# The first norm's shift and scale in four steps of two chunks each, on one core

## The chip, the cores and the metric

The kernel runs on one core of a Trainium2 chip. The metric is the device time of one execution in microseconds (us). It was run three times: 2135.63, 2139.49 and 2140.38 us, a median of 2139.49. One more execution was recorded by the hardware profiler; all rows below are from it.

## The reference

Two blocks follow one another; the change lies at the very start of the first. There a vector per stream (x and ctx) is turned into shifts and scales by a dense layer with 6144 outputs, the input is normed, scaled and shifted, and then multiplied by the mixer's input weights:

```python
m = jax.nn.silu(cvec) @ w_ada[:, :n * D_MODEL] + b_ada[:n * D_MODEL]
sh1, sc1, gt1, sh2, sc2, gt2 = jnp.split(m, 6, axis=-1)      # per stream
hx = rms_norm(h_x, g_mix) * (1.0 + sc1) + sh1                 # 256 x 1024, the same for ctx
proj = hx @ w_in                                              # 1024 x 2576
```

`D_MODEL` is 1024, x and ctx have 256 rows each. Only `sh1` and `sc1`, the first 2048 of the 6144 outputs, are needed for this first norm. Behind it follow a depthwise convolution, a state-space scan, an output projection and a mixture of experts, twice, and then a second block of four layers.

## The kernel before, in words

Features lie on the 128 partitions, so a stream is 8 chunks of 128 features by 256 rows; x and ctx stand side by side, 512 columns.

Shift and scale come from `w_ada` in units (`ada`, L200). A unit is one load of 1 MiB, 128 rows of `w_ada` by 2048 outputs, rows of 8 KB, and four fp32 matmuls (`adaps`) of 32 output rows by 512 columns that lie beside each other in the array; only two of the 32 rows are used (the two streams). Eight units add up to one block of 2048 outputs, and the first block is `sh1` and `sc1`. Then `turn` copies the sums from PSUM to `adar`, transposes them (`adat`) and makes `AD` (the vectors with their bias) and `A` (1 + scale, times the norm's gain). There are three blocks per layer and two layers, 48 units; `fill(n)` works off the next n of them, and its calls lie all over the first block wherever TensorE had room.

`load_x` (L162) loads the parameters, starts the first units, loads x and ctx, sums the squares (`ssq`, by matmuls with ones) with further units between them, takes root and reciprocal (`rs`), and works off the eighth unit and `turn`.

`mixer` (L304) loads the small `wd` weights and the first two pieces of `w_in`. All weights come by SyncE's queue into the tag `raw`, which has five buffers of 1 MiB: a load waits until the tile that had the buffer before has been read for the last time. Weights are split for fp32r into `wh` (ScalarE, L54) and `wl` (VectorE, L55). `modulated` (L279) then goes over the 8 chunks: times `rs` (`nrm`), times `A` plus `AD` (`nrmf`; VectorE for x, ScalarE for ctx), split into `xh` and `xl`. With each chunk `first` issues eight matmuls of 512 columns: two for `tmw`, and three each for the two projections that are open. These are the 64 first-stage matmuls. Further projections and the convolutions follow.

The order within each engine is made by a scheduler from the order of the program and priorities, and is fixed when the kernel is built; an engine takes its instructions in that order. It also hands out the `raw` buffers as they come free.

Of the kernel before, what the change touches and what calls it, by code (L numbers as in the profile page):

```python
# [7 lines left out]
F32 = mybir.dt.float32  # L8
# [3 lines left out]
AF = mybir.ActivationFunctionType  # L12
ALU = mybir.AluOpType
# [3 lines left out]
P = 128  # L17
D = 1024
KC = D // P
# [10 lines left out]
class Net:  # L30
# [100 lines left out]
    def block1(self):  # L131
        nc, tc, i = self.nc, self.tc, self.i
        with ExitStack() as c1:
            self.c1p = c1.enter_context(tc.tile_pool(name="consts1", bufs=1))
            self.consts()
            cb = ExitStack()
            self.big = cb.enter_context(tc.tile_pool(name="big", bufs=1))
            self.hs = [self.x, self.big.tile([P, KC, T], F32, name="hc")]
            self.AD = [self.c1p.tile([P, 48, 2], F32, name=f"AD{l}") for l in range(2)]
            self.A = [self.c1p.tile([P, 2, KC, 2], F32, name=f"A{l}") for l in range(2)]  # L140
            self.PV = [None, None]
            self.adar = self.c1p.tile([P, 4, P], F32, name="adar")
            self.turns, self.units = [], 0
            self.adag = [self.ada(0), self.ada(1)]
            self.moe_dram(c1, 2 * T)
            for l in range(2):
                with ExitStack() as c2:
                    self.tmp = c2.enter_context(tc.tile_pool(name="tmp", bufs=1))
                    self.pm = c2.enter_context(tc.tile_pool(name="pm", bufs=8, space=PSUM))
                    self.mmtag, self.t2b = "mm", 5  # L150
                    if l == 0:
                        self.load_x()
                    self.mixer(l)
                    if l:
                        self.setup2()
                if l == 0:
                    self.moe0(128)
            cb.close()
            self.b8p = self.ctx.enter_context(tc.tile_pool(name="b8", bufs=1, side="right"))
            self.moe1()  # L160

    def load_x(self):  # L162

        nc, i = self.nc, self.i
        c16 = self.params(0)
        sc = self.tmp.tile([P, 16], F32, name="silc")
        nc.scalar.activation(sc, c16, AF.Silu)
        self.sc32 = self.c1p.tile([P, KC, 32], F32, name="sc32")
        nc.gpsimd.memset(self.sc32, 0.0)
        nc.vector.tensor_copy(self.sc32[:, :, 0:2], sc.rearrange("p (s k) -> p k s", s=2))  # L170
        self.fill(2)
        for s, name in enumerate(("x", "ctx")):
            nc.sync.dma_start(self.hs[s], i[name])
        self.ssq_begin(2)
        for k in range(KC):
            self.ssq_add(k)
            if k % 2:
                self.fill(1)
        r = self.rs1 = self.rsn[:, :2 * T]
        nc.scalar.activation(r, self.ssq, AF.Sqrt, bias=self.eps[:, 0:1], scale=1.0 / D)  # L180
        with self.tc.high_priority(offset=-60):
            for q in range(4):
                nc.vector.reciprocal(r[:, q * P:q * P + P], r[:, q * P:q * P + P])
        self.fill(2)
        self.ada_flush()

    def params(self, l):

# [11 lines left out]
    def ada(self, l):  # L200

        nc, i = self.nc, self.i
        w = i["w_ada"][l].rearrange("(k p) n -> p k n", p=P)
        AD, A, rows = self.AD[l], self.A[l], self.adar

        def turn(b):  # L210
            pv = self.PV[l]
            pt = self.pm.tile([P, 4, P], F32, name="adat", tag=self.mmtag)
            for j in range(4):
                nc.tensor.transpose(pt[:, j], rows[:, j], self.ident)
            pt = pt.rearrange("p j (a r) -> p a j r", r=32)
            o = AD[:, 16 * b:16 * b + 16].rearrange("p (a j) s -> p a j s", j=4)
            for a in range(4):
                nc.vector.tensor_tensor(o[:, a], pt[:, a, :, 0:2], pv["b_ada"][:, 16 * b + 4 * a:16 * b + 4 * a + 4, None].to_broadcast([P, 4, 2]), op=ALU.add)
            if b != 1:
                n, at, gn = (0, 8, "g_mix") if b == 0 else (1, 32, "g_ffn")  # L220
                nc.vector.scalar_tensor_tensor(A[:, n], AD[:, at:at + 8], 1.0, pv[gn][:, :, None].to_broadcast([P, 8, 2]),
                                               op0=ALU.add, op1=ALU.mult)

        for b in range(3):
            ps, taken = None, False
            for k in range(KC):
                self.ada_flush()
                first = ps is None
                if first:
                    ps = self.pm.tile([P, 512], F32, name="adaps", tag=self.mmtag)  # L230
                r = self.raw(w[:, k, 2048 * b:2048 * b + 2048].rearrange("p (g n) -> p g n", n=512), 4, 512)
                for a in range(4):
                    self.mm(ps[32 * a:32 * a + 32], self.sc32[:, k], r[:, a], first, k == KC - 1)
                if k == KC - 1 or self.hold:
                    o = rows.rearrange("p j n -> p (j n)")
                    if taken:
                        nc.vector.tensor_tensor(o, o, ps, op=ALU.add)
                    else:
                        nc.scalar.activation(o, ps, AF.Copy)
                    ps, taken = None, True  # L240
                if k == KC - 1:
                    self.turns.append((turn, b))
                yield
# [32 lines left out]
        self.nc.scalar.activation(r, self.ssq, AF.Sqrt, bias=self.eps[:, 0:1], scale=1.0 / D)  # L276
        self.nc.vector.reciprocal(r, r)

    def modulated(self, l, which, streams, out_f=None, each=None, xs=None):  # L279

        nc = self.nc
        n = T * streams
        r = self.rs1
        xh, xl = xs or (self.b16("xh"), self.b16("xl"))
        for k in range(KC):
            t = self.tmp.tile([P, n], F32, name="nrm", tag="t2", bufs=self.t2b)
            f = self.tmp.tile([P, n], F32, name="nrmf", tag="t2", bufs=self.t2b) if out_f is None else out_f[:, k, :n]
            for s in range(streams):
                sl = slice(s * T, s * T + T)
                shift, scale = self.vec(l, 3 * which, k, s), self.A[l][:, which, k, s:s + 1]  # L290
                (nc.gpsimd if s else nc.vector).tensor_tensor(t[:, sl], self.hs[s][:, k], r[:, sl], op=ALU.mult)
                if s:
                    nc.scalar.activation(f[:, sl], t[:, sl], AF.Identity, bias=shift, scale=scale)
                else:
                    nc.vector.tensor_scalar(f[:, sl], t[:, sl], scale, shift, op0=ALU.mult, op1=ALU.add)
            self.split(xh[:, k, :n], xl[:, k, :n], f, nc.gpsimd if streams == 1 else None)
            if each:
                each(k, xh, xl)
        return xh, xl
# [1 line left out]
    def b16(self, name, dt=F32R, shape=None):  # L301
        return self.big.tile(shape or [P, KC, 2 * T], dt, name=name, tag="b16", bufs=5)

    def mixer(self, l):  # L304
        nc, i = self.nc, self.i
        last = l == 1
        NS = 1 if last else 2
# [10 lines left out]
        pt = self.pm.tile([32, 4 * P], F32, name="tmw", tag="mm")  # L318

        def first(k, xh, xl):  # L320
            self.mm(pt, wd[:, k], xh[:, k], k == 0, False)
            self.mm(pt, wd[:, k], xl[:, k], False, k == KC - 1)
            for q in range(2):
                self.mm3(p0[q], w0[q][0][:, k], w0[q][1][:, k], xh[:, k, :NX], xl[:, k, :NX], k == 0, k == KC - 1)
        xh, xl = self.modulated(l, 0, 2, each=first)
        pv = self.PV[l]

        pd = self.turned(pt, 16, 4, self.pm, self.tmp, "mm")
# [3 lines left out]
        a = self.tmp.tile([P, 16], F32, name="aneg")  # L332
# [31 lines left out]
        for c in range(4):  # L364
            b = c % 2
# [9 lines left out]
        for a in range(4):  # L375
            r = self.raw(win[:, :, 1536 + 256 * a:1792 + 256 * a], KC, 256)
            for b in range(2):
                c = 2 * a + b
# [34 lines left out]
            for k in range(k0, k1):  # L413
                self.mm3(ps[m], ws[m][0][:, k], ws[m][1][:, k], mh[:, k, :NX], ml[:, k, :NX], k == 0, k == KC - 1)
        if last:
            self.fill(48 - self.units, True)
            self.ada_flush()
        for m in range(3):
            wout(m, 0, 4)
# [182 lines left out]
    def ssd(self, l, xbc, xdt, cz, dt, dta, rows, NS, ssq, conv, cnorm):  # L602
# [116 lines left out]
        while todo or live or later:  # L719
            if todo:  # L720
                live.insert(0, head(n, *todo.pop(0)))
            live = [g for g in live if next(g, self) is not self]
            while sums:
                sums.pop(0)()
            if next(before, self) is self and later:
                s, c = later.pop(0)
                if s == 0:
                    carry(c)
                sums.append(finish(s, c))
            if n < half:  # L730
                conv(8)
            elif n == half:
                conv(1000)
            else:
                next(cnorm, None)
            if l == 0 and n in (12, 14):
                self.fill(1, n == 14)
            if l == 1 and self.units < 48:
                self.fill(1, self.units == 47)
            n += 1  # L740
        for f in sums:
            f()
# [1548 lines left out]
```

## Time and profile before

| | |
|---|---|
| median of 3 runs | 2139.49 us |
| the profiled execution | 2133.34 us, span 2131.5 us |
| TensorE (PE) busy | 1963.7 us, 92% of the span |
| VectorE (DVE) busy | 1472.7 us, 69% |
| ScalarE (ACT) busy | 1036.9 us, 49% |
| mean DMA rate | 192 GB/s |
| granted TensorE clock, mean | 0.967 of 2.4 GHz |

Shares over the whole span tell little of the change, which lies in the first 55 us. To read it one goes by stretches: which engine is full in which, and what ended the idle time ahead of the first matmuls of each kind. A clock of 0.50 is 1.2 GHz, 1.00 is 2.4 GHz. In the timeline a row merges instructions of one kind that follow one another (x8: eight of them), and an fp32 matmul leaves two records, an fp32r matmul one.

### The profile page before, as it was taken

The page shows a single profiled execution, that of the slowest core. Times are in us where ns is not written, and L with a number is a line of the kernel's source. Part 1 is how long each engine was busy: PE and PEld are TensorE (multiplying, and loading weights), DVE is VectorE, ACT ScalarE, POOL GpSimd, SP SyncE. Part 2 cuts the span into 40 slices and gives each one's busy share as a digit, 9 for nine tenths or more (in the row PEclk, how much of TensorE's full clock was granted, in tenths as well). Part 3 has the DMA queues.
Part 4 walks back from the last instruction along what each step waited for, and adds up shares of the span by engine and source line. Part 5 has one row for each costly group of instructions (what it writes and reads, how often), then busy time and mean ns, then how long its engine had stood idle before and what let it go on. Part 6 is the DMA issues. An engine that isn't in the chain of part 4 may idle for free.

```text
span 2131.5 us, 37017 instructions
## 1 busy us (share of the span) xinstructions
PE 1963.7 (92%) x14915; PEld 1696.5 (80%) x14915; DVE 1472.7 (69%) x2429; ACT 1036.9 (49%) x1742; POOL 437.1 (21%) x574
## 2 busy tenths in 40 slices
PE   6999786999889879799999997899999999999998
PEld 3666465998666656378889996799999999989998
DVE  4999558998796541089866679875558556767554
ACT  4335635886634521066554451354455444655444
POOL 1001202234251110113279812200010000010000
PEclk9999997999999989999999998899999999999999
DMA  7665236999326579955555552355544554436551
GB/s 304 232 207 172 82 103 221 346 339 335 109 73 236 178 245 368 378 173 179 172 185 184 198 177 93 110 187 189 192 138 153 190 191 161 139 108 218 189 179 40
DMA packets 275571, 408.89 MB, mean 192 GB/s; under 512 B 9856, under 2 KB 241280, under 8 KB 268096
## 3 DMA queue, kind: packets, MB, share of 16 engines
q1 hardware_dynamic: 265952, 380.47, 52.5%
q0 software_dynamic: 8000, 19.67, 2.6%
q10 hardware_dynamic: 1440, 6.29, 0.7%
q8 instruction: 120, 1.97, 0.4%
q14 instruction: 59, 0.48, 0.1%
HBM read 390.93 MB, written 24.64 MB: 195 GB/s over the span
## 4 chain that ended last, share of the span: by engine, by line
PE 48%; DVE 9%; DMA 2%; issue 2%; ACT 1%; POOL 1%; SPq 0%; DVEq 0%; POOLq 0%; ACTq 0%
PE mm L46 43%; DVE wl L55 2%; PE gu L46 2%; PE py L46 1%; DVE Z L2137 1%; DMA rawe<-in_w_down 1%; PE px L46 1%; DVE gl L1533 1%; DMA raw<-in_w_down 1%; DVE A L2130 0%; PE mm L1766 0%; DVE A L2139 0%; DVE s5a L2088 0%; POOL Z L2132 0%; DMA bc<-bcd 0%
## 5 line engine op out<-in xcount | busy, mean ns | idle before, releaser
L54 ACT ACTIVATE wh<-raw 128x1024 fp32r<-128x1024 f32 x490 | 511.2, 1050 | 477.8 <-PE mm L46 262.5
L55 DVE TENSOR_TENSOR wl<-raw,wh 128x1024 fp32r<-128x1024 f32 (+2 forms) x478 | 586.7, 1233 | 211.8 <-ACT wh L54 209.7
L46 PE MATMUL mm<-gh,wh 128*128 128x256 f32 (+1 forms) x1744 | 496.1, 285 | 1.0 <-ACT wh L54 1.0
L46 PE MATMUL mm<-gh,wl 128*128 128x256 f32 (+1 forms) x1744 | 493.0, 283 | 2.3 <-DVE wl L55 2.3
L46 PE MATMUL mm<-gl,wh 128*128 128x256 f32 (+1 forms) x1744 | 492.8, 283 | 0.5 <-DVE gl L1533 0.5
L46 PEld LDWEIGHTS mm<-gh,wh 128*128 128x128 f32 (+1 forms) x1744 | 329.0, 189 | 4.1 <-issue 1.8
L46 PEld LDWEIGHTS mm<-gh,wl 128*128 128x128 f32 (+1 forms) x1744 | 328.5, 188 | 3.7 <-DVE wl L55 3.0
L46 PEld LDWEIGHTS mm<-gl,wh 128*128 128x128 f32 (+1 forms) x1744 | 328.7, 188 | 2.3 <-DVE gl L1533 0.9
L46 PE MATMUL mm<-fh,wh 128*128 128x256 f32 x704 | 198.4, 285 | 3.1 <-DVE x L1573 1.6
L46 PE MATMUL mm<-fl,wh 128*128 128x256 f32 x704 | 198.8, 283 | 0.2 <-DVE fl L55 0.2
L46 PE MATMUL mm<-fh,wl 128*128 128x256 f32 x704 | 198.1, 283 | 0.0
L1537 POOL TENSOR_TENSOR sq<-sq 128x256 f32<-128x256 f32 x48 | 41.2, 859 | 682.2 <-ACT sq L1535 483.3
L46 PEld LDWEIGHTS mm<-fh,wh 128*128 128x128 f32 x704 | 133.6, 191 | 5.1 <-DVE x L1573 2.4
L46 PEld LDWEIGHTS mm<-fl,wh 128*128 128x128 f32 x704 | 134.7, 191 | 0.7 <-DVE fl L55 0.6
L46 PEld LDWEIGHTS mm<-fh,wl 128*128 128x128 f32 x704 | 134.5, 191 | 0.0
L46 PE MATMUL proj<-xh,wl 128*128 128x512 f32 (+1 forms) x320 | 117.6, 368 | 10.7 <-POOL xr L518 8.8
L46 PE MATMUL proj<-xh,wh 128*128 128x512 f32 (+1 forms) x320 | 119.3, 373 | 1.6 <-ACT wh L54 1.6
L46 PE MATMUL proj<-xl,wh 128*128 128x512 f32 (+1 forms) x320 | 116.3, 364 | 0.0
L46 PE MATMUL gu<-wh,gt 128*128 128x256 f32 x512 | 98.6, 286 | 0.2 <-DVE gt L55 0.2
L1599 DVE TENSOR_TENSOR ft<-mm,rstd 128x512 f32<-128x512 f32 x88 | 60.8, 691 | 51.0 <-PE mm L46 51.0
L54 ACT ACTIVATE fh<-fa 128x256 fp32r<-128x256 f32 x88 | 36.7, 417 | 111.6 <-DVE fa L1602 111.6
L46 PEld LDWEIGHTS proj<-xh,wh 128*128 128x128 f32 x320 | 63.1, 197 | 29.6 <-issue 15.9
(596 smaller groups left out, 4112.7 us busy)
## 6 DMA issues: line engine op xcount, KB each, us to landing
raw<-in_ffn_w_gate_up SPq DMA_DIRECT2D x88, 1024.0 KB, 5.4
raw<-in_w_ada SPq DMA_DIRECT2D x48, 1024.0 KB, 6.0
raw<-in_ffn_w_down SPq DMA_DIRECT2D x44, 1024.0 KB, 4.8
raw<-in_fox_w_in SPq DMA_DIRECT2D x24, 1024.0 KB, 6.2
raw<-in_w_down SPq DMA_DIRECT2D x22, 1024.0 KB, 11.2
raw<-in_w_in SPq DMA_DIRECT2D x20, 1024.0 KB, 5.4
raw<-in_w_gate SPq DMA_DIRECT2D x20, 1024.0 KB, 9.9
raw<-in_w_up SPq DMA_DIRECT2D x20, 1024.0 KB, 11.2
```

The lines of the kernel that those rows point to most:

```text
L46: return self.nc.tensor.matmul(out, a, b, start=start, stop=stop, skip_group_check=True)
L54: self.nc.scalar.activation(hi, src, AF.Copy)
L55: (lo_eng or self.nc.vector).tensor_tensor(lo, src, hi.bitcast(F32), op=ALU.subtract)
L1533: nc.vector.scalar_tensor_tensor(self.gl[:, k], x, s, self.gh[:, k].bitcast(F32), op0=ALU.mult, op1=ALU.subtract)
L1537: nc.gpsimd.tensor_tensor(sq, sq, self.sq, op=ALU.add)
L1599: nc.vector.tensor_tensor(t, gu, rs[:, None, :].to_broadcast([P, 2, T]), op=ALU.mult)
L2137: nc.vector.tensor_tensor_scan(z, self.rtab[:, 4 * m:4 * m + 4].rearrange("p a t -> p (a t)"), z, 0.0, ALU.mult, ALU.add)
```

## The change

The first block of units of layer 0 goes. In its place `ada_first` has four steps. Step j takes 256 outputs of the shift and the 256 of the scale that belong to chunks 2j and 2j + 1: two loads of 1 MiB (1024 rows of `w_ada` by 256 outputs, so rows of 1 KB), 32 matmuls of 32 output rows by 128 columns, one copy to `adar`, one transpose, and the `AD` and `A` of these two chunks. `load_x` issues the loads of step 0, then those of x and ctx, the squares, step 0 itself and the loads of step 1; `modulated` calls the next step ahead of chunks 2, 4 and 6, which works the step off and issues the next one's loads. The other 40 units stay where they were.

```diff
-        self.fill(2)
+        parts = self.ada_first()
+        next(parts)
...
-            if k % 2:
-                self.fill(1)
...
-        self.fill(2)
-        self.ada_flush()
+        next(parts)
+        return parts
+
+    def ada_first(self):
+        nc, l = self.nc, 0
+        w = self.i["w_ada"][l].rearrange("(k p) n -> p k n", p=P)
+        AD, A = self.AD[l], self.A[l]
+        for j in range(4):
+            rs = [self.raw(w[:, :, D * t + 256 * j:D * t + 256 * j + 256], KC, 256) for t in range(2)]
+            yield
+            pv = self.PV[l]
+            ps = self.pm.tile([P, P], F32, name="adaps", tag="mm")
+            for k in range(KC):
+                for a in range(4):
+                    self.mm(ps[32 * a:32 * a + 32], self.sc32[:, k], rs[a // 2][:, k, a % 2 * P:a % 2 * P + P], k == 0, k == KC - 1)
+            row = self.adar[:, j]
+            nc.scalar.activation(row, ps, AF.Copy)
+            pt = self.pm.tile([P, P], F32, name="adat", tag="mm")
+            nc.tensor.transpose(pt, row, self.ident)
+            pt = pt.rearrange("p (t c r) -> p t c r", t=2, r=32)
+            for t in range(2):
+                at = slice(8 * t + 2 * j, 8 * t + 2 * j + 2)
+                nc.vector.tensor_tensor(AD[:, at], pt[:, t, :, 0:2], pv["b_ada"][:, at, None].to_broadcast([P, 2, 2]), op=ALU.add)
+            nc.vector.scalar_tensor_tensor(A[:, 0, 2 * j:2 * j + 2], AD[:, 8 + 2 * j:10 + 2 * j], 1.0,
+                                           pv["g_mix"][:, 2 * j:2 * j + 2, None].to_broadcast([P, 2, 2]), op0=ALU.add, op1=ALU.mult)
...
-        for b in range(3):
+        for b in range(l == 0, 3):
...
         for k in range(KC):
+            if before:
+                before(k)
...
-        xh, xl = self.modulated(l, 0, 2, each=first)
+        xh, xl = self.modulated(l, 0, 2, each=first, before=(lambda k: k in (2, 4, 6) and next(parts, None)) if l == 0 else None)
...
-            self.fill(48 - self.units, True)
+            self.fill(40 - self.units, True)
```

TensorE before, from the last four units on; `sc` is the activated vector, `wd` the small weights, `proj` the two open projections:

```order
L46 MATMUL adaps<-raw,sc_127 32x512 x16
L214 MATMUL adat<-ident,adar 128x128 x4
L46 MATMUL tmw<-xh,wd_232 32x512
L46 MATMUL proj<-xh,wh 128x512
L46 MATMUL tmw<-xl,wd_232 32x512
L46 MATMUL proj<-xl,wh 128x512
L46 MATMUL proj<-xh,wl 128x512
L46 MATMUL tmw<-xh,wd_232 32x512
```

From here on 64 matmuls of `tmw` and `proj` follow with nothing between them. TensorE now, from the last matmuls of chunk 1 to the first of chunk 2:

```order
L46 MATMUL proj<-xl,wh 128x512
L46 MATMUL proj<-xh,wl 128x512
L46 MATMUL adaps<-raw,sc_127 32x128 x32
L203 MATMUL adat<-ident,adar 128x128
L46 MATMUL adaps<-raw,sc_127 32x128 x2
L46 MATMUL tmw<-xh,wd_219 32x512
L46 MATMUL proj<-xh,wh 128x512 x2
L46 MATMUL tmw<-xl,wd_219 32x512
```

The 32 matmuls of step 1 and its transpose now stand between chunks 1 and 2, with the first two matmuls of step 2 behind them; steps 2 and 3 stand in the same way ahead of chunks 4 and 6. Step 0 stands behind all eight `ssq` matmuls.

SyncE before, from the sixth unit's load to the first two pieces of `w_in`; `PE_49` is a wait for TensorE, `DVE_49` one for VectorE, `DMAHW` ones are for earlier transfers:

```order
L63 DMA raw_196<-in_w_ada 128x2048 [waits DMAHW1_49,DMAHW0_49,PE_49]
L63 DMA raw_207<-in_w_ada 128x2048 [waits DMAHW2_49,PE_49]
L63 DMA raw_213<-in_w_ada 128x2048 [waits DMAHW5_49,PE_49]
L63 DMA raw_230<-in_vec0 128x128 [waits DMAHW6_49,DMAHW3_49,PE_49]
L63 DMA raw_235<-in_w_in 128x8x256 [waits DMAHW7_49,DMAHW4_49,PE_49]
L63 DMA raw_237<-in_w_in 128x8x256 [waits DMAHW0_49,PE_49]
```

SyncE now, from the weights `wd` on (the loads of steps 0 and 1, x and ctx are ahead of these and wait for nothing):

```order
L63 DMA raw_217<-in_vec0 128x128
L214 DMA pv1_1542<-in_vec1 128x324 [waits DMAHW0_49]
L1526 DMA cols_7183<-in_vec2 128x106 [waits DMAHW1_49]
L63 DMA raw_222<-in_w_in 128x8x256 [waits DMAHW7_49,DMAHW2_49,DVE_49]
L63 DMA raw_224<-in_w_in 128x8x256 [waits DMAHW3_49,PE_49]
L63 DMA raw_310<-in_w_ada 128x8x256 [waits DMAHW4_49,PE_49]
L63 DMA raw_312<-in_w_ada 128x8x256 [waits DMAHW5_49,PE_49]
L63 DMA raw_385<-in_w_ada 128x8x256 [waits DMAHW6_49,PE_49]
L63 DMA raw_387<-in_w_ada 128x8x256 [waits DMAHW4_49,PE_49]
```

The first piece of `w_in` now waits for VectorE's split of `wd`, the second for TensorE, and so do the four loads of steps 2 and 3: `raw_224` and `raw_310` take the buffers of step 0, `raw_312` and `raw_385` those of step 1, `raw_387` one of step 2.

## Rows read from the trace of the kernel before

**Rows 1.** Busy time by stretches; TensorE's granted clock, DMA share, GB/s at the end.
```profile
5.00:10.00 5.00, 2.84 (x16) 0.54 (x16) 2.06 (x16) 0.00 (x0) 0.00 (x0) 1.00 1.01 424
20.00:25.00 5.00, 5.00 (x24) 1.51 (x16) 0.00 (x0) 0.66 (x1) 0.00 (x0) 1.00 1.02 424
31.00:33.00 2.00, 0.05 (x1) 0.00 (x0) 1.81 (x8) 0.90 (x2) 0.98 (x2) 1.00 1.05 336
35.00:41.00 6.00, 5.12 (x13) 3.01 (x12) 6.00 (x8) 4.36 (x8) 2.08 (x3) 0.50 1.02 399
56.00:160.00 104.00, 104.00 (x496) 70.35 (x495) 98.81 (x207) 34.89 (x48) 1.18 (x16) 1.00 0.65 226
```

**Rows 2.** TensorE in order of time: start, duration, work [idle ahead of it, releaser].
```profile
14.06 5.40 PE L46 MATMUL ssq<-sq,ones 128*128 128x512 f32 x8 [3.26 <-ACT sq L270]
...
24.26 1.02 PE L46 MATMUL ssq<-sq,ones 128*128 128x512 f32 x2
...
28.61 1.06 PE L46 MATMUL adaps<-raw,sc 128*32 128x512 f32 x8 [0.62 <-DMA raw<-in_w_ada]
...
34.72 0.42 PE L46 MATMUL tmw<-xh,wd 128*32 128x512 f32 x1 [3.67 <-ACT xh L54]
...
37.30 0.63 PE L46 MATMUL proj<-xh,wl 128*128 128x512 f32 x1
37.72 0.63 PE L46 MATMUL tmw<-xh,wd 128*32 128x512 f32 x1
...
52.87 0.40 PE L46 MATMUL proj<-xl,wh 128*128 128x512 f32 x1
53.11 0.39 PE L46 MATMUL proj<-xh,wl 128*128 128x512 f32 x1
```

**Rows 3.** ScalarE in order of time, the same columns, from 28 to 36 us.
```profile
28.80 0.31 ACT L54 ACTIVATE wd<-raw 128x128 fp32r<-128x128 f32 x1 [2.80 <-DMA raw<-in_vec]
...
32.10 1.09 ACT L293 ACTIVATE nrmf<-nrm,AD,A 128x256 f32<-128x256 f32 x2 [1.77 <-DVE A L221]
33.10 1.04 ACT L54 ACTIVATE wh<-raw 128x1024 fp32r<-128x1024 f32 x1
...
35.71 0.63 ACT L54 ACTIVATE xh<-nrmf 128x512 fp32r<-128x512 f32 x1
```

**Rows 4.** Instructions on tiles `adat` and `AD`: ns least/median/most, first and last start.
```profile
L214 PE MATMUL adat<-ident,adar x24: 270/272/346, 30.4 to 714.2; 128*128 128x128 f32 x24
L218 DVE TENSOR_TENSOR AD<-adat,pv x24: 155/157/167, 31.1 to 716.2; 128x8 f32<-128x8 f32 x24
L221 DVE SCALAR_TENSOR_TENSOR A<-AD,pv x4: 166/171/503, 31.5 to 716.2; 128x16 f32<-128x16 f32 x4
```

**Rows 5.** TensorE in order of time in the S5 stage, strips of 32.
```profile
1289.67 1.05 PE L46 MATMUL mm<-A,bc 128*32 128x128 f32 x32
1290.54 1.05 PE L46 MATMUL mm<-B,bc 128*32 128x128 f32 x32
```

**Rows 6.** SyncE's waits to 55 us: us in total, times, longest.
```profile
SPq L63 <- PE adaps L46: 15.2, 8, 4.4
```

**Rows 7.** DMA issues from 55.2 to 55.7 us: size, us to landing.
```profile
raw<-in_w_in SPq DMA_DIRECT2D x1, 1024.0 KB, 5.3
```

**Rows 8.** Stretches as in rows 1, around two changes of the clock.
```profile
14.00:18.00 4.00, 3.94 (x5) 1.65 (x6) 0.00 (x0) 2.51 (x9) 0.00 (x0) 0.57 1.01 426
41.50:42.00 0.50, 0.50 (x3) 0.40 (x2) 0.50 (x2) 0.10 (x1) 0.15 (x1) 0.66 1.04 341
```

More of the change, by code (lines that the diff above doesn't have):

```diff
@@ L151, in block1 @@
                     if l == 0:
-                        self.load_x()
-                    self.mixer(l)
+                        parts = self.load_x()
+                    self.mixer(l, parts)
                     if l:
@@ L277, in ssq_end, with modulated @@
         self.nc.vector.reciprocal(r, r)
-    def modulated(self, l, which, streams, out_f=None, each=None, xs=None):
+    def modulated(self, l, which, streams, out_f=None, each=None, xs=None, before=None):
         nc = self.nc
@@ L302, in b16, with mixer @@
         return self.big.tile(shape or [P, KC, 2 * T], dt, name=name, tag="b16", bufs=5)
-    def mixer(self, l):
+    def mixer(self, l, parts):
         nc, i = self.nc, self.i
@@ L737, in ssd @@
                 self.fill(1, n == 14)
-            if l == 1 and self.units < 48:
-                self.fill(1, self.units == 47)
+            if l == 1 and self.units < 40:
+                self.fill(1, self.units == 39)
             n += 1
```

## The prediction

> **What bounds the kernel now.** I read the busy time by stretches first [rows 1]. From 5 to 41 us the DMA engines are full (share 1.01 to 1.05): this is the stage that the change touches, in which 8 MiB of `w_ada`, x, ctx and two pieces of `w_in` come in. From 45 us on it turns: in 56 to 160 us TensorE is busy 104.00 of 104.00 us at the full clock and VectorE 98.81 of 104. Everything in that stretch needs the first projections, so whatever moves their end moves the rest with it. Second, TensorE in order of time [rows 2]: the sums of squares run from 14.06 us, the last unit of the norm's vectors ends at 28.61 + 1.06 = 29.67, the first matmul on a modulated chunk starts at 34.72 after an idle 3.67 put down to `xh`, and the last of the 64 first-stage matmuls ends at 53.11 + 0.39 = 53.5 us. That moment is what I forecast. Third, SyncE's queue [rows 6]: it waited 15.2 us for the `adaps` matmuls to give back buffers, but always with other loads still on their way, since the DMA engines stayed full.
>
> **What stays, what moves.** Before, 8 units are worked off while the DMA runs, the vectors are ready once, and then 64 matmuls run in one piece. After, by the order of TensorE's instructions, it reads: 8 sums of squares, step 0, 16 matmuls (chunks 0 and 1), step 1, 16, step 2, 16, step 3, 16. TensorE takes its instructions in that order, so three steps now stand between projections, each followed by a wait for its own result. The five `raw` buffers matter as much: steps 0 and 1 and the small `wd` weights fill them, so the second `w_in` piece and the first load of step 2 go out only after step 0, the second load of step 2 and the first of step 3 after step 1, and the last load after step 2.
>
> **The sum, by the moment at which the 64 matmuls end.**
>
> Sums of squares. Before they take 14.06 to 24.26 + 1.02 = 25.28 us, 11.22 us, with two `adaps` units of 1.06 inside [rows 2]: 9.1 us of their own. The two loads ahead of x and ctx now have rows of 1 KB. Where `w_in`, which has such rows, came in, 336 GB/s were moved at a full share, against 424 for `w_ada` in rows of 8 KB [rows 1]: two MiB cost 6.2 us and not 4.9, so x and ctx land 1.3 us later. 15.4 + 9.1 = 24.4 us (23.2 if the shorter rows cost nothing; 25.9 if the low clock at their start lasts as long as from 35 us, below).
>
> The Trainium skill, "DMA: Bandwidth & Descriptors", section "Specifications", puts the least transfer for line rate at 512 B; by it 1 KB rows would come as fast as 8 KB rows. The trace's 336 against 424 GB/s differs, and I go by the trace; by the rule this term is 1.3 us smaller.
>
> Step 0. 32 matmuls of 32 output rows by 128 columns, which the trace before does not have in this place. The nearest row is the S5 stage, with strips of the same shape: 32 records (an fp32 matmul leaves two) start 0.87 us before the next 32 and last 1.05 [rows 5]. A step is 64 records: 1.75 to 2.1, taken as 1.9 us; 26.3. At half the clock it would be 3.6.
>
> To the first chunk. The second `w_in` piece is issued at 26.4 and lands 5.3 us later, as such a load did into an idle queue [rows 7]: 31.7. On ScalarE the order is the split of both `w_in` pieces, then the modulation: 1.04 for the split, 1.09 for two `nrmf`, 0.63 for `xh` [rows 3]: the first matmul starts at 34.5 us, against 34.72. Starting the modulation after 2 MiB instead of 8 thus gains 0.2 us (1.4 at best, a loss of 1.3 at worst, by the bounds above), for the sums of squares and the weights of the projection hold it, not the vectors.
>
> Chunks 0 and 1. Matmuls are 0.24 us apart at the full clock (52.87 to 53.11) and 0.42 at the low one (37.30 to 37.72) [rows 2]. TensorE stands idle before, so they begin low: before, it was 1.2 GHz for most of the 3.9 us from 14.06 to 18 [rows 8] and for about 7 us after the start at 34.72 (0.50 to 41, 0.66 in 41.5 to 42) [rows 1, 8]. I take 5.4 us: 13 matmuls low and 3 full, 6.2 us (5.5 to 6.8); 40.7.
>
> Then three times the same. A step, 1.9. A wait: the end of the step to `adar` 0.07, its copy 0.31 (the 128x128 copy of `wd` [rows 3]; it is a quarter of before's), the transpose 0.27, two `AD` of 0.16 and one `A` of 0.17 [rows 4], hand-overs between engines of some 0.04 to 0.09 five times, two `nrmf` 1.09, `xh` 0.63: 3.0 us. Nothing hides it, since all that TensorE has next is the chunk that waits; only the transpose and two matmuls of the following step lie in it. It could be 2.4 if `xh` waited for one `nrmf` only, and 4.0 by the nearest stretch of before (29.67 to 34.72, less the 1.04 of a weight split). Before pays such a wait once. Then 16 matmuls at 0.235, 3.7 us. The loads keep up: the two loads behind step 1 are issued at 42.6 and land at 47.9 and 51.0, for steps that start at 49.3 and 57.9; the last is issued at 51.2 and lands at 56.5. So 3 x (1.9 + 3.0 + 3.7) = 25.8, and the end is 40.7 + 25.8 = 66.5 us.
>
> 66.5 - 53.5 = +13.0 us. By parts: start -0.2, less time at the low clock -1.9 (the 64 took 18.8 us before; now 6.2 and 11.1), three steps +5.7, three waits +9.0; together +12.6, the rest is rounding. Bounds: 33.3 + 5.5 + 3 x (1.75 + 2.4 + 3.7) = 62.4, +8.9; and 36.0 + 6.8 + 3 x (2.1 + 4.0 + 3.7) = 72.2, +18.7.
>
> Behind it. The rest of `w_ada` is worked off in the same number of units at the same places, and the loads for the next projections (two units, two `w_in` pieces) go out at 51 to 62 us, before they are needed. I count nothing for that, and nothing is given back, as TensorE has no idle in 56 to 160 us.
>
> The profiled execution took 2133.34 us with a span of 2131.5; it would take 2146.3. The median of the runs is 2139.49, 6.15 above it, and I forecast that: 2139.49 + 13.0 = 2152.5 us.
>
> **Rivals.**
>
> The clock falls in every wait. TensorE idles about 3 us three times, and before, the clock was at 0.57 in 14 to 18 us, behind an idle of 3.26, and at 0.50 from 35 us, behind one of 3.67 [rows 1, 2, 8]. Then the pairs cost 6.8 and the steps 3.6: 34.5 + 6.8 + 3 x (3.6 + 3.0 + 6.8) = 81.5, +28.0, 2167.5 us; with one fall of the three about 2157. Against it: now each wait has 10 us of matmuls before it, and in the waits fall a transpose and a bit of the next step. Chance 0.22.
>
> The Trainium skill, "TensorE: Matmul & The Clock Gate", section "HAM oscillation — how this bites in real kernels", tells of short bursts of matmuls with waits for DMA between them, where every burst began at the low clock; by that rule this rival would be the result. The trace shows such a fall after two idles, none as part of a row of bursts.
>
> Faster: the vectors' loads are what ends last, as the share of 1.01 to 1.05 says. If buffers didn't hold the loads back, the 12.4 MiB of the stage would be in by about 40 us (8 MiB of `w_ada` and 2 of `w_in` at 336 GB/s, 31.2 us, x and ctx at 424, 4.9, the small ones 1.2, from 2.5 us on), with all earlier chunks done beside them, and only one step, wait and pair would follow: 40 + 1.9 + 3.0 + 3.7 = 48.6, -4.9, 2134.6 us. It decides if each step's loads are there before the pair ahead is done and the waits lie under the DMA. Against it: the loads go out one step late, and the first chunk starts at 34.5. Chance 0.08.
>
> No change: the lost time is given back behind the stage, 2139.5 us. For it, TensorE idles here and there after 160 us; against it, the stretch right behind is full on TensorE and nearly so on VectorE. Chance 0.05.
>
> **How the numbers follow.** Forecast 0.65, clock rival 0.22, faster 0.08, no change 0.05. 0.2% is 4.3 us, about the least that a measurement of this kernel can tell. Slower by more: 0.87; within: 0.05; faster: 0.08. The likeliest case alone spans 2148 to 2158. The range has to take in most of the clock rival, so it ends at 2167; below, it starts at 2145, leaving out the two other cases.
>
> **What would show it.** Right: in TensorE's order of time three idles of about 3 us before a `tmw`, released by ScalarE's `xh`, each behind a step of some 2 us; the last first-stage matmul near 66 us; the DMA share well under 1 between 22 and 50 us; SyncE waiting for `adaps`. Wrong: a first `tmw` well before 33 us, waits under 2 us, or an end of the stage later than 53.5 that is gone by 160 us. A granted clock of 0.50 past 42 us would show the clock rival.

## The result, and the profile after

The changed kernel takes 2158.18 us (median of 4 runs, 2157.01 to 2160.18) against 2137.56 for the kernel before in the same comparison (4 runs, 2133.04 to 2140.38): ratio 1.0103, 95% interval 1.0087 to 1.0119, +20.6 us. The forecast was 2152.5 in 2145 to 2167. The sign came as forecast, and so did the steps and the waits; the shift was forecast as +13.0 and is half as large again, because something was added that the forecast had given to a rival, the low clock behind each wait. The time lies in the range since that had been stretched for this rival: the likeliest case alone was to span 2148 to 2158. The profiled execution took 2159.0 us with a span of 2157.2.

TensorE in order of time in the changed kernel (start, duration, work, idle ahead of it and its releaser), the lines that answer to [rows 2]:

```profile
15.55 9.78 PE L46 MATMUL ssq<-sq,ones 128*128 128x512 f32 x16 [15.55 <-ACT sq L294]
25.27 1.96 PE L46 MATMUL adaps<-raw,sc 128*32 128x128 f32 x64
...
35.63 0.64 PE L46 MATMUL tmw<-xh,wd 128*32 128x512 f32 x1 [7.66 <-ACT xh L54]
37.57 0.64 PE L46 MATMUL tmw<-xl,wd 128*32 128x512 f32 x1 [1.30 <-DVE xl L55]
...
42.90 1.96 PE L46 MATMUL adaps<-raw,sc 128*32 128x128 f32 x64
45.28 0.33 PE L203 MATMUL adat<-ident,adar 128*128 128x128 f32 x1 [0.42 <-ACT adar L201]
45.54 0.41 PE L46 MATMUL adaps<-raw,sc 128*32 128x128 f32 x4
47.83 0.42 PE L46 MATMUL tmw<-xh,wd 128*32 128x512 f32 x1 [1.88 <-ACT xh L54]
...
49.34 0.63 PE L46 MATMUL proj<-xl,wh 128*128 128x512 f32 x1
49.77 0.63 PE L46 MATMUL proj<-xh,wl 128*128 128x512 f32 x1
...
52.96 0.39 PE L46 MATMUL proj<-xh,wl 128*128 128x512 f32 x1
53.28 1.94 PE L46 MATMUL adaps<-raw,sc 128*32 128x128 f32 x60
...
58.15 0.42 PE L46 MATMUL tmw<-xh,wd 128*32 128x512 f32 x1 [1.88 <-ACT xh L54]
...
63.56 1.94 PE L46 MATMUL adaps<-raw,sc 128*32 128x128 f32 x60
...
68.43 0.43 PE L46 MATMUL tmw<-xh,wd 128*32 128x512 f32 x1 [2.22 <-ACT xh L54]
...
73.51 0.40 PE L46 MATMUL proj<-xh,wl 128*128 128x512 f32 x1
```

The pattern is the forecast one: a step of 1.94 to 1.96 us, an idle released by `xh`, sixteen matmuls, three times over. Each step starts right behind the pair ahead, with no idle, so none of them waited for its loads. From the end of a step to the first `tmw` it is 47.83 - 44.86 = 2.97 us, then 2.93 and 2.93; a transpose lies inside, and in the first two also four records of the next step. The stage ends at 73.51 + 0.40 = 73.91 us, against 53.50 before: +20.4 us, which is the whole of the +20.6. By parts: the first `tmw` 0.9 later (35.63 against 34.72), three steps 5.8, three waits 8.8, and the 64 matmuls themselves 4.8 (7.27 + 5.45 + 5.41 + 5.48 = 23.6 against 18.8 before). This last part was not forecast, and most of it is inside the pairs: the matmuls start 0.43 us apart up to 51.48 (49.34 to 49.77) and 0.23 to 0.24 apart after it (16 of them 47.83 to 53.28, the next step's start).

What fills one wait, on ScalarE and then on VectorE, the same columns:

```profile
44.95 0.28 ACT L201 ACTIVATE adar<-adaps 128x128 f32<-128x128 f32 x1 [8.85 <-PE adaps L46]
46.17 1.09 ACT L319 ACTIVATE nrmf<-nrm,AD,A 128x256 f32<-128x256 f32 x2 [0.94 <-DVE A L208]
47.16 1.13 ACT L54 ACTIVATE xh<-nrmf 128x512 fp32r<-128x512 f32 x2
```

```profile
45.64 0.23 DVE L207 TENSOR_TENSOR AD<-adat,pv 128x4 f32<-128x4 f32 x2 [7.53 <-PE adat L203]
45.91 0.16 DVE L208 SCALAR_TENSOR_TENSOR A<-AD,pv 128x4 f32<-128x4 f32 x1
```

No link of that chain is longer than half a microsecond but the modulation (two `nrmf` and `xh`); the engines pass it on one after the other, and TensorE, whose next work in order needs the last of them, has nothing else.

Stretches of the changed kernel (busy time of each engine, granted clock of TensorE, DMA share, GB/s), to be held against [rows 1]:

```profile
35.00:40.00 5.00, 3.07 (x7) 2.08 (x8) 3.12 (x4) 1.10 (x3) 2.71 (x3) 0.50 0.02 4
...
45.00:50.00 5.00, 2.84 (x11) 1.59 (x12) 3.53 (x9) 2.36 (x5) 1.25 (x2) 0.82 0.83 263
50.00:55.00 5.00, 5.00 (x71) 3.66 (x70) 0.00 (x0) 0.00 (x0) 0.27 (x1) 0.84 0.51 161
55.00:60.00 5.00, 2.74 (x17) 1.45 (x11) 3.52 (x9) 2.41 (x5) 0.78 (x1) 0.85 0.81 265
...
75.00:80.00 5.00, 5.00 (x26) 3.38 (x23) 4.06 (x8) 4.92 (x8) 0.00 (x0) 1.00 0.64 195
```

The same columns for the first matmul of chunk 2 and for a stretch behind it:

```profile
47.83:48.09 0.26, 0.26 (x1) 0.22 (x2) 0.26 (x1) 0.26 (x1) 0.26 (x1) 1.00 1.09 390
48.50:51.00 2.50, 2.50 (x7) 1.50 (x6) 0.95 (x2) 0.00 (x0) 0.74 (x1) 0.50 1.10 360
```

Before, the DMA engines were full up to 41 us. Now their share is 0.02 in 35 to 40 and 0.00 in 40 to 45, because the loads of the later steps wait for buffers that the earlier steps hold, and 0.37 to 0.83 in the slices from 45 to 75. The clock, which before came back at 42 us and stayed, is below 1 in every such slice from 35 to 75 us. It does not fall inside the wait: in each of the three pairs the first matmul still runs at the full clock, then 1.2 GHz shows (0.50), and the full clock is back some 3.6 us into the pair (at 51.48 in the first).

**Behind the stage.** The median says that all of the loss is in the stage. The profiled executions say more: 2159.0 - 2133.34 = +25.7, of which +20.4 is there at 54 us, +22.8 at 280, +24.0 at 960 and +25.7 at the end (medians, over a stretch, of how much later each VectorE instruction starts than the same one before). One place where it grows, TensorE before and then after:

```profile
244.91 0.65 PE L46 MATMUL py<-es,xdt 128*64 128x256 f32 x4 [2.83 <-DVE es L699]
```

```profile
264.25 1.12 PE L46 MATMUL py<-es,xdt 128*64 128x256 f32 x4 [2.83 <-DVE es L725]
```

The same work behind the same idle of 2.83 us, at the full clock in one and at the low clock in the other (granted 1.00 in 244 to 245.6 us before, 0.50 in 263.4 to 265.5 after). Whether this belongs to the change is tested below.

### The profile page after: what moved, and what is told of

It reads as the page before. It is cut to its first block, busy times and chain, and to the rows that moved or that the text cites. A ratio compares the mean times of both kernels' runs of the same rounds, so it can differ in the third digit from the quotient of the medians.

```text
span 2157.2 us, 37413 instructions
## 1 busy us (share of the span) xinstructions
PE 1966.0 (91%) x15103; PEld 1703.1 (79%) x15107; DVE 1473.2 (68%) x2436; ACT 1037.3 (48%) x1745; POOL 436.7 (20%) x574
## 4 chain that ended last, share of the span: by engine, by line
PE 47%; DVE 9%; DMA 2%; issue 2%; ACT 1%; POOL 1%; SPq 0%; DVEq 0%; POOLq 0%; ACTq 0%
PE mm L46 42%; DVE wl L55 3%; PE gu L46 2%; PE py L46 1%; DVE Z L2163 1%; DMA raw<-in_w_down 1%; DMA rawe<-in_w_down 1%; DVE gl L1559 1%; PE px L46 1%; DVE A L2156 0%; PE mm L1792 0%; DMA bc<-bcd 0%; DVE A L2165 0%; DVE s5a L2114 0%; POOL Z L2158 0%
## 5 line engine op out<-in xcount | busy, mean ns | idle before, releaser
L46 PEld LDWEIGHTS proj<-xh,wh 128*128 128x128 f32 x320 | 63.3, 198 | 29.6 <-issue 16.6
```

Of the source, the lines that this page charges most:

```text
L46: return self.nc.tensor.matmul(out, a, b, start=start, stop=stop, skip_group_check=True)
```

## The experiments

Theory A: the steps and waits of the forecast, and the low clock behind the waits, make the stage longer. B: loads and buffers set the pace. C: the pairs are slow for another reason. "Stage end" is the end of the last of the 64 matmuls, 53.5 before and 73.9 after. Behind each ratio stands its 95% interval; the difference is against the median of the kernel before in the same comparison.

**Each step one pair ahead.** Step j + 1 is issued before the pair that needs step j.

```
-  before=(lambda k: k in (2, 4, 6) and next(parts, None))
+  before=(lambda k: k in (0, 2, 4) and next(parts, None))
```

> The changed kernel with each step worked off one pair of chunks earlier: step 1 ahead of chunk 0, step 2 ahead of chunk 2, step 3 ahead of chunk 4; loads, matmuls and buffers are the same. Theory A (the 20.4 us that the first stage grew are three steps of 2.0, three waits of 3.0 for a step's own result, and a low clock of 1.7 behind each wait): the waits lie under a pair's matmuls and go, and with them the low clock behind them; only the steps stay. First tmw at 35.6 as in the changed kernel, the last first-stage matmul at 59 to 61 us instead of 73.9, total 2143 to 2147 us. Theory B (the loads, held by the five buffers and slower in rows of 1 KB, set the pace, and where the steps stand matters little): the stage ends at 70 us or later, total 2154 or more.

2143.11 us (7 runs), ratio 1.0036 [1.0024, 1.0047], +9.4; stage end 58.96. TensorE, and two stretches:

```profile
42.57 1.95 PE L46 MATMUL adaps<-raw,sc 128*32 128x128 f32 x64
44.46 0.42 PE L46 MATMUL tmw<-xh,wd 128*32 128x512 f32 x1
...
44.95 0.33 PE L203 MATMUL adat<-ident,adar 128*128 128x128 f32 x1
```

```profile
45.00:55.00 10.00, 9.89 (x97) 6.80 (x96) 5.09 (x15) 4.06 (x9) 0.80 (x1) 1.00 0.80 270
55.00:60.00 5.00, 4.97 (x26) 3.24 (x30) 1.93 (x4) 2.90 (x4) 0.00 (x0) 1.00 0.84 301
```

Behind step 2 the next `tmw` follows at once, and the step's chain runs beside the pair. The waits are gone, the clock is 1.00 from 45 us on, and the stage is 5.5 us later than before: 1.5 at the start (first `tmw` at 36.24) and two steps of 1.95 inside the stage. Theory A holds for 15 of the 20.4 us. The weights still went through the same five buffers, which speaks against B; they did start earlier, as each buffer was given back a pair sooner, but in the changed kernel no step had waited for them.

**The waits filled.** Two needless fp32 matmuls (four records) behind the transpose of steps 1 to 3.

```
+  if j:
+      pd = self.pm.tile([P, 512], F32, name="warm", tag="mm")
+      for q in range(2):
+          self.mm(pd, self.ones, self.MA.rearrange("p a n -> p (a n)"), q == 0, q == 1)
```

> The changed kernel with two fp32 matmuls of 128x512 on constants, whose result nobody reads, behind the transpose of steps 1, 2 and 3, so that TensorE has 1.7 us of work in each wait of 1.9; nothing else is moved. Theory A: the low clock behind each wait is a result of TensorE's idle time; with the idle filled the 16 matmuls of a pair take 3.7 us instead of 5.4, the waits keep their 3.0, the stage ends at 68 to 70 us instead of 73.9 and the total falls by 4 to 6 us. Rival C (the pairs are slow for another reason, as xl or the loads arriving late): the pairs stay at 5.4 us and the stage ends at 73.9 or later.

2157.81 us (4 runs), ratio 1.0099 [1.0082, 1.0116], +24.1; stage end 68.77, 5.1 us earlier than after.

```profile
44.28 1.88 PE L46 MATMUL warm<-MA,ones 128*128 128x512 f32 x4
46.09 0.41 PE L46 MATMUL adaps<-raw,sc 128*32 128x128 f32 x4
46.67 0.42 PE L46 MATMUL tmw<-xh,wd 128*32 128x512 f32 x1 [0.17 <-ACT xh L54]
...
50.88 1.94 PE L46 MATMUL adaps<-raw,sc 128*32 128x128 f32 x60
```

```profile
45.00:50.00 5.00, 4.65 (x20) 2.44 (x19) 3.14 (x6) 2.13 (x4) 1.52 (x2) 1.00 1.03 339
```

From the step to the `tmw` it takes 46.67 - 43.68 = 2.99 us as before, so the chain is not touched; the clock stays at 1.00 and the three pairs take 4.21, 4.21 and 3.93 in place of 5.45, 5.41 and 5.48. This shows that the slow half of each pair is the clock (against C). The pairs account for 4.0 of the 5.1 us; the other 1.2 were won ahead of the first filler, where step 1 ended at 43.68 and not at 44.86. The total shows none of it: the 5.1 us went again behind the stage.

**All four steps ahead of `w_in` and of every chunk.** A single run, so it is read by its stage and not by its total.

```
-  next(parts)
+  for _ in parts:
+      pass
```

> The four steps as in the change (loads in rows of 1 KB, 32 matmuls by 128 columns each, one transpose each), but all of them worked off before the first chunk, and the pieces of w_in loaded behind them; no step stands between chunks. Theory A: the 64 matmuls run in one piece again, 16 to 19 us, behind one wait; only the loads, which the buffers hold back by a step each, delay their start to 46 to 48 us: end at 64 to 66 us. Theory B (the loads alone set the pace): the end is at 73.9 or later, as the loads are the same and come no earlier.

2145.72 us, +12.0; stage end 60.79, 3 to 5 us sooner than expected.

```profile
33.40 3.22 PE L46 MATMUL adaps<-raw,sc 128*32 128x128 f32 x60 [2.90 <-DMA raw<-in_w_ada]
...
39.36 1.94 PE L46 MATMUL adaps<-raw,sc 128*32 128x128 f32 x60 [1.58 <-DMA raw<-in_w_ada]
...
44.24 0.60 PE L46 MATMUL tmw<-xh,wd 128*32 128x512 f32 x1 [0.95 <-DVE AD L208]
```

Here the loads do set the pace up to the start of the last step at 39.36: steps 2 and 3 wait for their weights. The 64 matmuls then run in one piece in 16.6 us (18.8 before). One pass of loads and one wait cost less than three waits: this order is the nearest to that of before, and 13 us better than the changed one in the stage.

**The steps' loads freed from the buffers.** Steps 1 to 3 get buffers of their own and are loaded early; the order of the work stays.

```
+  rb = self.b16("adab", F32)
+  rs = [rb[:, :, 256 * t:256 * t + 256] for t in range(2)]
```

> The changed kernel with the loads of steps 1 to 3 put into other buffers that are free at this time, all issued early (step 0, x, ctx, step 1, the small weights, both w_in pieces, steps 2 and 3), so that none waits for a step; steps and chunks stand as in the change, but the matmuls of steps 2 and 3 move into the waits ahead of chunks 2 and 4, since their data are there. Theory A: the first tmw comes at 30 to 32 us since w_in no longer waits for step 0; the three waits of 3.0 us stay, but two of the three steps lie inside them: end of the stage at 57 to 61 us, total 2141 to 2146. Theory B (the loads set the pace): all 12.4 MiB are in by about 40 us, and the stage ends at 48 to 51 us, total 2132 to 2136.

2148.38 us (4 runs), ratio 1.0057 [1.0041, 1.0074], +14.7; stage end 65.39, so 8.5 us won and not the 13 to 17 expected, and far from theory B's 48 to 51.

```profile
43.58 1.94 PE L46 MATMUL adaps<-adab,sc 128*32 128x128 f32 x60
45.87 0.41 PE L46 MATMUL tmw<-xh,wd 128*32 128x512 f32 x1 [0.35 <-ACT xh L54]
...
58.89 0.33 PE L217 MATMUL adat<-ident,adar 128*128 128x128 f32 x1 [0.37 <-ACT adar L215]
61.44 0.42 PE L46 MATMUL tmw<-xh,wd 128*32 128x512 f32 x1 [2.22 <-ACT xh L54]
```

```profile
60.00:65.00 5.00, 3.56 (x16) 2.53 (x16) 2.24 (x5) 2.88 (x6) 0.00 (x0) 1.00 0.01 2
```

With its weights there, step 2 is laid into the wait behind step 1, so two of the steps cost little. The chain behind each step still has to be waited for, as I had expected. What I had wrong is the start, 34.49 us for the first `tmw` and not 30 to 32, and the rest of the stage, 30.9 us where 27 to 29 were expected: the last two records and the transpose of steps 2 and 3 stand behind the pair, and those waits became 3.3 us (58.11 to 61.44). The third idle is as long as in the changed kernel, 2.22 us, and there the clock did not fall (1.00). So a wait of this length is not enough to lower it each time. Counted over these runs, idles of 1.9 to 2.2 us ahead of a pair were followed by a fall six times of seven (both profiles of the changed kernel, and this one), and waits that were filled, here (the first two) and in the run with the waits filled, none of five times.

**x and ctx first, free loads, steps ahead of chunks 1, 3 and 5**: the version that these results point to.

```
-  before=(lambda k: k in (2, 4, 6) and next(parts, None))
+  before=(lambda k: k in (1, 3, 5) and next(parts, None))
...
   for s, name in enumerate(("x", "ctx")):
       nc.sync.dma_start(self.hs[s], i[name])
+  parts = self.ada_first()
+  next(parts)
```

> The steps kept, with what the first runs point to: x and ctx are loaded ahead of step 0's weights, the weights of steps 1 to 3 have buffers of their own and are loaded right behind w_in, and each step is issued one chunk earlier (ahead of chunks 1, 3 and 5). Theory A (steps, the waits behind them and the clock): squares from about 7 us, sums end at 17, first tmw at 27 to 30 (10 us behind the sums, as with the free loads), then the 22.7 us that the run with the step one pair ahead took from its first tmw to its last proj, plus one more step inside (1.96): stage end 51 to 55 against 53.5, and 2131 to 2139 with what is lost later. Rival B (loads set the pace): 12 MB at the 348 GB/s of the steps' loads end at about 37 us; if step 3 waits for them beside the rest, the last pair starts at 43 and the stage ends at 47 to 48: 2126 to 2131.

2141.04 us (11 runs), ratio 1.0025 [1.0014, 1.0036]; stage end 55.87. Against before it loses 5.5 us where the changed kernel loses 20.6, so it beats the one and not the other. Both are above what theory A gave (51 to 55, 2131 to 2139), and B's 47 to 48 did not come.

```profile
29.26 0.63 PE L46 MATMUL tmw<-xh,wd 128*32 128x512 f32 x1 [7.97 <-ACT xh L54]
...
33.34 2.02 PE L46 MATMUL adaps<-adab,sc 128*32 128x128 f32 x64
```

```profile
25.00:30.00 5.00, 0.63 (x1) 0.13 (x1) 4.06 (x7) 2.24 (x4) 3.01 (x4) 0.50 1.09 348
30.00:35.00 5.00, 4.78 (x67) 3.64 (x71) 0.77 (x2) 0.00 (x0) 0.74 (x1) 0.65 1.10 349
```

The first chunk starts 5.5 us sooner than before, and the stage still ends 2.4 later: three steps of 2 us and waits of half a microsecond to a microsecond lie inside it, which before lay under the loads.

**The same with steps ahead of chunks 0, 2 and 4.**

```
-  before=(lambda k: k in (1, 3, 5) and next(parts, None))
+  before=(lambda k: k in (0, 2, 4) and next(parts, None))
```

> As the run with x and ctx loaded first, with the steps ahead of chunks 0, 2 and 4 in place of 1, 3 and 5: step 1 falls into the wait of 8.0 us that TensorE has there between step 0 and the first tmw (20.97 to 29.26). Theory A: step 1 (1.96) costs nothing there if its weights have landed by about 25 (8 MB at 348 GB/s), so the stage ends 2 us or more sooner than the 55.7 of that run, at 51 to 54, and the total falls by as much, 2136 to 2140. Rival: its weights land after 27, and the first tmw waits behind the step: stage end 55 to 57, 2140 to 2143. Either is within what the clock later on gives or takes, so the stage is to be read for it.

2143.43 us (5 runs), ratio 1.0035 [1.0021, 1.0048]; stage end 56.28. The rival came true (its total 0.4 us above what it gave):

```profile
24.13 0.64 PE L46 MATMUL adaps<-adab,sc 128*32 128x128 f32 x4 [3.63 <-DMA adab<-in_w_ada]
27.16 3.63 PE L46 MATMUL adaps<-adab,sc 128*32 128x128 f32 x60 [2.39 <-DMA adab<-in_w_ada]
```

Step 1 waited for its weights to 27.16 and then ran at the low clock, 3.63 us for 60 records.

**Only x and ctx first, in the kernel before.**

```
-  self.fill(2)
   for s, name in enumerate(("x", "ctx")):
       nc.sync.dma_start(self.hs[s], i[name])
+  self.fill(2)
```

> The kernel before with one thing moved: x and ctx are loaded ahead of the first two units' weights, in place of behind them. Theory A: the squares start at about 7 us in place of 11.1, but the shift and scale still need all 8 units' weights and w_in comes behind them, so the first tmw (34.7) moves by no more than the reciprocals and norms that can now be done ahead of the last unit: 32 to 35, total 2130 to 2137, within 2 us of before. Rival B (the late sums of squares held the stage): first tmw at 30 or earlier, 4 us or more gained.

2136.01 us (12 runs) against 2135.54 (26 runs), ratio 1.0000 [0.9989, 1.0011]: no change. But it did not test what it was meant to test:

```profile
12.39 1.94 PE L46 MATMUL adaps<-raw,sc 128*32 128x512 f32 x8 [12.39 <-DMA raw<-in_w_ada]
14.25 2.08 PE L46 MATMUL ssq<-sq,ones 128*128 128x512 f32 x2
...
36.78 0.64 PE L46 MATMUL tmw<-xh,wd 128*32 128x512 f32 x1 [4.63 <-ACT xh L54]
```

In TensorE's order a unit still stands ahead of the squares, and its weights now came at 12.39. So the squares started at 14.25 us, not at about 7 (14.06 before), and the first `tmw` came 2.1 us later than before, not at 32 to 35. Whether late sums of squares held the stage of before stays open.

**Only a delay.** What is lost behind the stage? The kernel before got 8 and 22 needless matmuls behind its first stage, 7.0 and 19.0 us long.

```
+  pw = self.pm.tile([P, 512], F32, name="warm", tag="mm")
+  for q in range(8):    # or 22
+      self.mm(pw, self.ones, self.MA.rearrange("p a n -> p (a n)"), q == 0, q == 7)
```

> The kernel before, unchanged but for 8 needless fp32 matmuls of 128x512 behind the first stage, 0.47 us a pass and two passes each as in the run with the filler: 7.5 us in which TensorE is busy, so that all that follows comes 7.5 us later. Theory D (what the changed kernel loses later, +2.5 us by 275 us and +5.3 by its end, comes with the time at which the later stages start: where the clock falls in their waits): the loss behind the stage is another one in this run than with 22 matmuls, anywhere from -1 to +6 us, total 2140 to 2147. Rival O (the scheduler lays the later instructions in another order as soon as the first stage is longer): the same loss in both, 4 to 6 us, here 2145 to 2147. Rival S (the loss belongs to the steps themselves, such as their buffers or loads): no loss, 2141 within 1.

> As the run with 8 needless matmuls, with 22: 20.7 us, about the 20.4 us by which the changed kernel leaves the stage later. Theory D: the loss behind the stage is near the changed kernel's +5.3, since all comes at nearly the same times as there, and not that of the run with 8: total 2157 to 2161. Rival O: the same loss as with 8. Rival S: no loss, 2154 within 1.

With 8: 2146.61 us (7 runs, 2141.87 to 2150.39), ratio 1.0046 [1.0032, 1.0059], +11.1. With 22: 2154.51 us (4 runs: 2153.33, 2153.74, 2155.29 and 2163.95), ratio 1.0081 [1.0063, 1.0099], +19.0. So the shorter delay lost 4 us behind the stage and the longer none, by the medians (11.1 - 7.0 and 19.0 - 19.0), which is not the 2157 to 2161 of theory D for the longer, nor the same loss in both of rival O; the profiled execution of the longer is the one of 2163.95, nearly 9 us above its next. The first 50 us of both are the kernel before unchanged, and even there the clock came back at other times, seen in the same stretch with 8 and then with 22:

```profile
40.00:45.00 5.00, 5.00 (x23) 3.70 (x22) 4.44 (x8) 2.59 (x5) 1.58 (x2) 1.00 0.79 253
```

```profile
40.00:45.00 5.00, 5.00 (x17) 3.51 (x16) 4.44 (x8) 2.46 (x5) 1.57 (x2) 0.71 0.77 248
```

**The changed kernel once more**, for a second profile.

> The changed kernel once more, on the chip of this call, for a second profile of the same program. Theory D (what is lost behind the stage is where the clock happens to fall): the stage ends near 73.9 again, and the loss behind it (+5.3 in the first profile) is another number, by 1 us or more in some stretch. Rival O (an order of instructions that costs the same each time): +5.3 within 0.5, in the same stretches.

2159.37 us (4 runs), ratio 1.0103 [1.0088, 1.0119], +21.5; profiled 2159.96, stage end 73.87.

How much later than in the profile of before the runs are, in us (with a delay, the stage end is that of the needless matmuls):

| kernel | stage end | at 280 | at 960 | end | median against before's |
|---|---|---|---|---|---|
| changed | 20.4 | 22.8 | 24.0 | 25.7 | +20.6 |
| changed, again | 20.4 | 22.8 | 24.0 | 26.6 | +21.5 |
| one pair ahead | 5.5 | 5.5 | 6.9 | 9.6 | +9.4 |
| waits filled | 15.3 | 17.6 | 21.7 | 24.6 | +24.1 |
| steps first | 7.3 | 6.5 | 9.7 | 12.4 | +12.0 |
| loads free | 11.9 | 12.5 | 11.9 | 14.8 | +14.7 |
| x first | 2.4 | 3.0 | 3.7 | 8.4 | +5.5 |
| x first, ahead | 2.8 | 1.9 | 8.2 | 10.0 | +5.6 |
| before, delay 7.0 | 6.4 | 5.8 | 9.1 | 11.7 | +11.1 |
| before, delay 19.0 | 19.7 | 19.1 | 29.2 | 30.6 | +19.0 |
| before, x first | 0.6 | -0.9 | 2.9 | 2.7 | +0.5 |

The last columns differ because the profile of before (2133.34) is a quick one: its medians in the comparisons are 2133.7 to 2137.8. In their profiles all runs but two drift by 3 us or more behind the stage, also the two delayed ones that have no step in them, by amounts that differ between two delays of one program (rival O, the same loss in both, falls) and, within limits, between executions. By the medians the drift runs from about nothing (changed kernel, longer delay) to 8.8 us (waits filled). Rival S, no loss without steps, fails with the shorter delay (2146.61 where it gave 2141), but the longer one's median is the 2154 that it gave. And the 26 executions of the unchanged kernel before in one comparison lie between 2131.15 and 2142.05, so drifts of a few us between two single profiles say little. The second profile of the changed kernel repeats the first up to 280 us and then wanders off by up to 2 us and back; there theory D held in part only, as some of the loss does repeat. The rows at 244.91 and 264.25 show the clock as one cause. It is not the only one: x first and loads free have a higher mean granted clock than before (0.970 against 0.967) and drift by 6.0 and 2.9 us all the same. Nor is it the order of the later instructions alone: by operations and tiles, steps first, loads free, both x first and before with x first have the same order on every engine behind the stage as before, and drift by 2.1 to 7.2 us; in the others 63 to 74 of VectorE's 2366 instructions stand elsewhere. What else is in it, and why the kernel with filled waits lost as much as it had won, stays open.

## Why the prediction was right in sign and short in size

Stage end forecast 66.5, measured 73.9, above the upper bound of 72.2 that the sum had; the total lies in its range through the part that was added for the rival. The 7.4 us by the terms of the sum:

- **Sums of squares**: forecast 15.4 + 9.1 = 24.4; measured 15.55 + 9.78, 25.3. The matmuls ran at the full clock (1.00 from 15.5 to 25 us) and still took 0.7 us longer than the 9.1 that were read from a stretch partly at the low one; why stays open. The start was right: loads with 1 KB rows are slower, as [rows 1] had it, and in the run with x first they moved 348 GB/s at a share of 1.09, where rows of 8 KB before had moved 424 at 1.01. The Trainium skill, "DMA: Bandwidth & Descriptors", section "Specifications", puts line rate at 512 B and up; with 348 against 424 GB/s this kernel's traces do not agree.
- **Start of the chunks**: forecast 34.5, measured 35.63; the 0.9 us of the sums is passed on to it by the second `w_in` piece. But the run with free loads had that piece early and still started at 34.49: there ScalarE's `nrmf` waited for GpSimd's `nrm`, and that for VectorE's reciprocals, with the weight splits between them.
- **Chunks 0 and 1**: forecast 6.2, measured 42.90 - 35.63 = 7.27. I had left out the 1.30 us that the second `tmw` waits for `xl`, behind the split of the second `w_in` piece on VectorE. Before has that idle too, 0.88 us, in a line between those of [rows 2].
- **Steps**: forecast 1.9, measured 1.94 to 1.96. Right, from the strips of another stage [rows 5].
- **Waits**: forecast 3.0, measured 2.97, 2.93, 2.93. Right, from single instructions and hand-overs, with some luck: the parts that the forecast names add up to 3.06 to 3.31, and in the trace some of them overlap (two `AD` take 0.23 together, the second `nrmf` ends behind the start of `xh`). The nearest whole stretch of before would have said 4.0.
- **Pairs at 3.7 us**: this is the step that failed. Measured 5.45, 5.41 and 5.48, together 5.2 of the 7.4 us. I had argued that ten microseconds of matmuls ahead of each wait, and a transpose in it, would keep the clock up. By my own terms there were only 6.2 + 1.9 = 8.1 us ahead of the first wait and 3.7 + 1.9 = 5.6 ahead of the others. The clock fell behind all three waits, just after the pair had begun, and in both profiles. In the forecast's sum by parts this is the term "less time at the low clock": 18.8 before against 6.2 + 11.1 is -1.5, not the -1.9 that stands there (with it the parts give the +13.0 and nothing is left to rounding), and +4.8 was measured.

The rival for this had a chance of 0.22 and +28.0 us. It was wrong in the other direction: it let the steps run low too and the pairs to their end, whereas the clock came back 3.6 us into each pair, so that each step (1.94) ran at the full clock. The truth lay between the two cases, so that 2158.18 fell in the range is in part luck. The sign that I had named for this rival, a granted clock of 0.50 past 42 us, is there in each pair. The filled waits showed that it is the clock; the pair ahead showed what goes when the wait goes.

The Trainium skill, "TensorE: Matmul & The Clock Gate", section "HAM oscillation — how this bites in real kernels", describes bursts of matmuls that each begin at the low clock because the engine waits between them. Here three bursts in a row turned slow right behind their first matmul, nearly as it says, though the waits were for other engines and not for DMA; the third wait of the run with free loads, as long, did not.

The other rivals: "the loads end last" needed free buffers, and with free loads and x first the stage came to 55.9, not 48.6, because the steps and their chains lie inside it. "Given back behind the stage" did not happen. I had counted nothing behind the stage, and by the medians that is what the change costs there (+20.6 against +20.4); by the profiles it was 5 us more, within what a mere delay of the kernel before brought (5.3 and, in its slowest execution, 10.9). That the medians agree so well is luck too: by theirs, other kernels of the table lose 3 to 9 us there.

## What to carry to other kernels

A value that many matmuls wait for is cheap to make once under the loads; made in pieces between the matmuls, each piece brings its own chain from TensorE through ScalarE and VectorE and back (here 2.95 us) and, where the clock falls behind it, another 1.7 us of slow matmuls. If it must be made in pieces, issue each one pair ahead: that took 15 of the 20.4 us back. And read a change in an early stage from that stage's end: behind it, this kernel drifts by several microseconds after a mere delay, and unchanged it took 2131.15 to 2142.05 us in the executions of one comparison.

## What was not expected of the hardware

- Behind the same idle of 2.83 us the clock was up in the kernel before and low in both profiles of the changed one (0.65 and 1.12 us for the same four records). Behind waits of 2.9 us it fell six times of six in the changed kernel, at nearly the same moments in both profiles, and not in the run with free loads. It fell not in the wait but with the work that followed.
- Matmuls as fillers in a wait of 3 us held the clock at 1.00 and took 1.2 to 1.6 us off the pair behind it.
- One program, executed four times on one chip, took 2153.33, 2153.74, 2155.29 and 2163.95 us.
